# The reciprocal roots of the norms: from ScalarE's square root to VectorE alone

## The chip, the cores and the metric

The kernel runs on one core of a Trainium2 chip. Five engines of that core work side by side, each through its own queue in order: TensorE (PE, matrix products into PSUM), VectorE (DVE), ScalarE (ACT), GpSimd (POOL) and SyncE (SP, which issues the transfers). The metric is the time of one launch on the device in microseconds; lower is better.

## The reference

Four transformer layers over 512 tokens of width 1024, batch 1, in float32. Layers 0 and 1 are a block with sparse attention (a top-k of keys, then compressed and selected keys) and a gated feed-forward network; layers 2 and 3 are a block with gated linear attention (GLA) and sliding-window attention, each with a squared-ReLU network of width 4096. What matters here is the norm that stands ahead of every product, behind some of them, and inside GLA:

```
def rms_norm(x, w):
    xf = x.astype(jnp.float32)
    y = xf * lax.rsqrt(jnp.mean(xf * xf, axis=-1, keepdims=True) + NORM_EPS)
    return (y * w.astype(jnp.float32)).astype(x.dtype)
```

For each token (or each token and head) it needs one number, the reciprocal root of a mean of squares.

## The kernel before

The activations are kept transposed: `x` is a tile of 128 partitions by 8 chunks by 512 tokens. Weights come from HBM in units of 128x1024, once each. A float32 product is made of three matmuls in the fast float32 form: weights and activations are split into a rounded part `hi` and a rest `lo` (`mm3`, L195; lines L198 to L200). So each unit of weights costs an ACT copy (`whi`, L188) and a subtraction (`wlo`, L175) on DVE or, where the caller says `eng=self.G`, on POOL, in pieces of 256 columns.

A norm goes in these steps. ACT squares the activations (L224), DVE adds them up (L226, L230), and a matmul with a column of ones sums over the partitions (`sums_out`, L235), so that the sum of each token stands in one partition, one column for each block of 128 tokens. `meanv` (L254, or L257, or by hand at L963 and L1409) makes the mean plus epsilon in a tile `mv` of 1 to 8 columns. `rsqrt` (L238) makes the reciprocal root in a tile `rsq`. Either the root is used as a factor for each partition, when a product is moved out of PSUM (L1042, L1110, L1620) or a tile is scaled (L794, L796), or `bcast` (L269) spreads it over all partitions: DVE multiplies it into an identity (L273), a matmul with ones copies it to every row (L277), and ACT moves that to SBUF as `rb` (L280).

`rsqrt` before: ACT takes the square root of `v` into a tile `rs_s` (L243), DVE takes the reciprocal (L244), and one Newton step on DVE sharpens it (L245 to L247): y becomes y times (1.5 - 0.5 v y y). The square root needs ACT's table of that function; ACT's other functions here with a table of their own are Exp, Silu, Tanh and Ln, and where the next function's table isn't there, a load of it (ACT_TABLE_LOAD) stands ahead of it in ACT's queue.

`rsqrt` is called 26 times in a run: for the memory's norm (L567) and the norm of `ckv` (L1105) in layer 0, ahead of every mixer and every network (through `rms`, L260, and at L765, L976), for both roots at the start of layer 2 (L1411), for each of GLA's four heads (L1615), behind the mixers and networks of layers 2 and 3 (`post_norm`, L818 and L821), and for the output rows at the very end (`result_of`, L964).

The order of the work is written by hand with `weave` and `steps`, which mix lists of steps in a given ratio. The final order of each engine's queue comes from a planner that lists the instructions by a simulated time line:

```
    with tile.TileContext(nc, schedule_with_timeline_sim=True) as tc:
        body(tc, args)
```

Of the kernel before, what the change touches and what calls it, by code (L numbers as in the profile page):

```python
# [9 lines left out]

F32 = mybir.dt.float32
F32R = mybir.dt.float32r
AF = mybir.ActivationFunctionType
ALU = mybir.AluOpType
AX = mybir.AxisListType

P = 128
# [92 lines left out]
class Core:  # L110
# [20 lines left out]
    def pair(self, name):  # L131

        return self.blk([P, 2, S], F32R, name)

# [42 lines left out]
    def split(self, src, hi, lo, eng=None):  # L177
        self.A.activation(hi, src, AF.Copy)  # L178
        self.lo(lo, src, hi, eng)
# [4 lines left out]
    def wunit(self, src, n=1024, eng=None):  # L184
        raw = self.wraw()
        hi, lo = (self.wp.tile([P, 1024], F32R, tag=t, name=self.uid(t), bufs=NW) for t in ("whi", "wlo"))
        self.nc.sync.dma_start(raw[:, :n], src)
        self.A.activation(hi[:, :n], raw[:, :n], AF.Copy)  # L188
        w = 256 if eng is self.G else 512
# [13 lines left out]
    def sums(self, srcs, sl=ALL, scale=None):  # L203
# [7 lines left out]
        else:  # L211
            for c, x in enumerate(srcs):
                o = self.t2() if c else acc
                self.A.activation(o[:, sl], x, AF.Square, scale=scale(c))
                if c:
# [3 lines left out]
    def sums_in(self, pairs, out, st=None, last=True):  # L219

        st = {} if st is None else st
        for x in pairs:
            o = self.t2([P, 2, 256])
            self.A.activation(o, x, AF.Square)  # L224
            if "a" in st:
# [11 lines left out]

    def rsqrt(self, v, n):  # L238

        s = self.sm([P, 16], "rs_s", 2)  # L240
        y = self.sm([P, 16], "rsq", 6)
        t = self.sm([P, 16], "rs_t", 2)
        self.A.activation(s[:, :n], v, AF.Sqrt)  # L243
        self.V.reciprocal(y[:, :n], s[:, :n])  # L244
        self.V.tensor_tensor(t[:, :n], y[:, :n], y[:, :n], ALU.mult)  # L245
        self.V.scalar_tensor_tensor(t[:, :n], t[:, :n], -0.5, v, ALU.mult, ALU.mult)
        self.V.scalar_tensor_tensor(y[:, :n], t[:, :n], 1.5, y[:, :n], ALU.add, ALU.mult)  # L247
        return y[:, :n]

    def meanv(self, ssum, n, dim, mul=None):  # L250
# [18 lines left out]
    def bcast(self, y, nb=NB, out=None):  # L269
# [8 lines left out]
        if out is None:  # L278
            out = self.sm([P, S], "rb", 2)[:, :n]
        self.A.activation(out, ps[:, :n], AF.Copy)  # L280
        return out
# [10 lines left out]
    def act_half(self, gain, sl):  # L292

        ts = [self.blk([P, 2, 2, 256], F32R, "ah") for _ in range(4)]
        out = [(ts[c // 2][:, c % 2, 0], ts[c // 2][:, c % 2, 1]) for c in range(KC)]
# [64 lines left out]
    def tr4(self, srcs, tag="gm"):  # L360

        ps = self.psum(tag, F32R)
        for j, x in enumerate(srcs):
# [3 lines left out]
    def stack_steps(self, jobs, tag="gm", eng=None, hi="A"):  # L367


        def task(*job):  # L370
# [3 lines left out]
            def s0():  # L374
                src = job[0][:] if len(job) == 3 else job[0][job[1]][:, b]
                v["st"] = st = self.t2([P, 4, 2, 64], F32R)
                src4 = src.rearrange("p (h d) -> p h d", d=64)
# [19 lines left out]
    def k_stack(self, src, out):  # L397

        sh, sl = self.t2([P, NB, 2, 64], F32R), self.t2([P, NB, 2, 64], F32R)
        src = src[:, :, None, :].to_broadcast([P, NB, 2, 64])  # L400
# [1492 lines left out]
```

## Time and profile before

| | us |
|---|---|
| median of 3 timed runs | 2369.89 |
| lowest and highest | 2369.83, 2370.73 |
| the profiled execution | 2373.13 |
| its span, first to last instruction | 2371.4 |

The profiled execution is one run of its own, taken with the profiler; all rows are of it. The page gives for each engine its busy time, its share of the span and its number of instructions. The mean granted clock of PE over the span is 0.992 of full speed. Rows of the timeline begin with the start and the duration in us, then engine, line, operation and tiles; an idle time of the engine before the instruction and what ended it stand in brackets at the end.

### The profile page before, as it was taken

To read this page: it belongs to the slowest core of one execution; us is meant where nothing else is said; L and a number is where in the kernel's file an instruction comes from. 1 tells how busy PE (TensorE), PEld (TensorE's weight loads), DVE (VectorE), ACT (ScalarE), POOL (GpSimd) and SP (SyncE) were. 2 spreads that over 40 slices of the span, in tenths; PEclk is the share of its full clock that TensorE was granted. 3 is DMA by queue.
4 is the path that set the end of the run, shared out by engine and by line. 5 is a ranking of instruction groups with operands and counts; after the bars stand their busy time and mean duration, and the time that the engine had idled before them with its cause. 6 is when DMAs were issued, how large, how long until landed. Compare 5 with 4: busy or idle time off the path is not lost.

```text
span 2371.4 us, 35348 instructions
## 1 busy us (share of the span) xinstructions
PE 2323.4 (98%) x13390; PEld 2006.0 (85%) x13390; DVE 1436.0 (61%) x2978; ACT 1130.5 (48%) x2121; POOL 476.2 (20%) x706
## 2 busy tenths in 40 slices
PE   8899999999999999999999999999999999999998
PEld 8788988888997879888888998988888877988886
DVE  5996655455667676555456446844446796644446
ACT  6677522222457675222226566633325686533233
POOL 2756000000137730000001660000000161000000
PEclk9999999999999999999999999999999999999999
DMA  5213422223330114222222214523234413522234
GB/s 179 72 37 101 145 101 93 98 98 98 101 132 21 58 43 141 98 98 98 98 94 77 81 63 149 171 92 104 89 104 154 146 61 125 167 87 102 97 98 142
DMA packets 68300, 243.88 MB, mean 103 GB/s; under 512 B 7569, under 2 KB 7825, under 8 KB 68130
## 3 DMA queue, kind: packets, MB, share of 16 engines
q1 hardware_dynamic: 68130, 241.62, 30.7%
q8 instruction: 106, 1.74, 0.3%
q14 instruction: 64, 0.52, 0.1%
HBM read 239.50 MB, written 2.10 MB: 102 GB/s over the span
## 4 chain that ended last, share of the span: by engine, by line
PE 89%; DVE 6%; ACT 3%; DMA 1%; issue 1%; POOL 0%; SPq 0%; DVEq 0%; ACTq 0%; POOLq 0%
PE ps L199 11%; PE ps L200 11%; PE ps L198 11%; PE tr L198 10%; PE tr L199 10%; PE tr L200 10%; PE gm L198 3%; PE gm L200 3%; PE gm L199 3%; PE acc L529 2%; PE more L198 2%; PE more L200 2%; PE more L199 2%; PE tr L451 2%; PE ps L424 1%; PE ps L425 1%
## 5 line engine op out<-in xcount | busy, mean ns | idle before, releaser
L188 ACT ACTIVATE whi<-raw 128x1024 fp32r<-128x1024 f32 (+1 forms) x443 | 466.4, 1054 | 863.0 <-PE ps L199 221.0
L175 DVE TENSOR_TENSOR wlo<-raw,whi 128x512 fp32r<-128x512 f32 x744 | 524.9, 747 | 322.9 <-ACT whi L188 321.4
L175 POOL TENSOR_TENSOR wlo<-raw,whi 128x256 fp32r<-128x256 f32 x284 | 219.7, 805 | 272.2 <-ACT whi L188 184.2
L200 PE MATMUL ps<-act,wlo 128*128 128x512 f32 (+1 forms) x712 | 257.1, 361 | 0.5 <-DVE wlo L175 0.4
L198 PE MATMUL ps<-act,whi 128*128 128x512 f32 (+1 forms) x712 | 257.0, 361 | 0.2 <-DVE m L863 0.2
L199 PE MATMUL ps<-act,whi 128*128 128x512 f32 (+1 forms) x712 | 256.8, 361 | 0.1
L200 PE MATMUL tr<-act,wlo 128*128 128x512 f32 (+1 forms) x640 | 231.7, 362 | 0.0
L198 PE MATMUL tr<-act,whi 128*128 128x512 f32 (+1 forms) x640 | 231.4, 362 | 0.2 <-ACT whi L188 0.2
L199 PE MATMUL tr<-act,whi 128*128 128x512 f32 (+1 forms) x640 | 231.3, 361 | 0.0
L731 POOL TENSOR_TENSOR sm_s<-sm_s,sm_s 128x512 f32<-128x512 f32 x40 | 51.6, 1289 | 532.0 <-DVE sm_s L730 532.0
L200 PEld LDWEIGHTS ps<-act,wlo 128*128 128x128 f32 x712 | 134.4, 189 | 21.1 <-DVE wlo L175 0.7
L198 PEld LDWEIGHTS ps<-act,whi 128*128 128x128 f32 x712 | 134.3, 189 | 20.8 <-issue 0.6
L199 PEld LDWEIGHTS ps<-act,whi 128*128 128x128 f32 x712 | 134.1, 189 | 20.7 <-DVE act L302 0.3
L198 PEld LDWEIGHTS tr<-act,whi 128*128 128x128 f32 x640 | 120.8, 189 | 18.7 <-ACT whi L188 0.3
L199 PEld LDWEIGHTS tr<-act,whi 128*128 128x128 f32 x640 | 120.9, 189 | 18.5
L200 PEld LDWEIGHTS tr<-act,wlo 128*128 128x128 f32 x640 | 120.8, 189 | 18.3
L445 POOL TENSOR_TENSOR sm_s<-sm_s,nm_r 128x256 f32<-128x256 f32 (+2 forms) x172 | 104.3, 622 | 50.8 <-DVE nm_r L479 19.3
L178 ACT ACTIVATE hid<-sm_s 128x512 fp32r<-128x512 f32 x88 | 55.7, 632 | 109.5 <-DVE sm_s L884 58.0
L198 PE MATMUL gm<-whi,act 128*128 128x256 f32 (+1 forms) x360 | 103.3, 289 | 1.3 <-ACT rb L280 0.6
L200 PE MATMUL gm<-whi,act 128*128 128x256 f32 (+1 forms) x360 | 102.6, 287 | 0.0
L199 PE MATMUL gm<-wlo,act 128*128 128x256 f32 (+1 forms) x360 | 102.1, 286 | 0.0
L199 PE MATMUL ps<-wlo,hid 128*128 128x512 f32 x256 | 99.7, 390 | 0.0
(661 smaller groups left out, 5803.8 us busy)
## 6 DMA issues: line engine op xcount, KB each, us to landing
raw<-in_w_down SPq DMA_DIRECT2D x124, 512.0 KB, 3.3
raw<-in_w_ffn SPq DMA_DIRECT2D x96, 512.0 KB, 3.3
raw<-in_w_up SPq DMA_DIRECT2D x80, 512.0 KB, 3.4
raw<-in_w_o SPq DMA_DIRECT2D x32, 512.0 KB, 3.3
raw<-in_w_glao SPq DMA_DIRECT2D x16, 512.0 KB, 3.4
raw<-in_w_swa SPq DMA_DIRECT2D x16, 512.0 KB, 3.3
raw<-in_w_swao SPq DMA_DIRECT2D x16, 512.0 KB, 3.3
raw<-in_w_dsa SPq DMA_DIRECT2D x14, 512.0 KB, 3.9
```

Source lines behind the costliest of these rows:

```text
L175: (eng or self.V).tensor_tensor(out, src, hi.bitcast(F32), ALU.subtract)
L178: self.A.activation(hi, src, AF.Copy)
L188: self.A.activation(hi[:, :n], raw[:, :n], AF.Copy)
L198: mm(out, l[0], r[0], start=start, stop=False)
L199: mm(out, l[0], r[1], start=False, stop=False)
L200: mm(out, l[1], r[0], start=False, stop=stop)
L424: self.T.matmul(out, q[:, t], k[0][:, k0:k0 + n], start=True, stop=False)
L425: self.T.matmul(out, q[:, t], k[1][:, k0:k0 + n], start=False, stop=True)
L445: self.G.tensor_tensor(p, p, r.to_broadcast([P, p.shape[-1]]), ALU.mult)
L451: self.T.transpose(ps[:, s], p[:, s], self.ident)
L529: return self.T.matmul(acc[e * 64:e * 64 + 64, t0:t0 + p[e].shape[-1]], v[e], p[e], start=start and i == 0, stop=stop and i == n - 1)
L731: self.G.tensor_tensor(u, u, t, ALU.mult)
```

## The change

`rsqrt` no longer uses ACT. DVE takes the bits of `v` as an integer, multiplies by -0.5 and adds 1597463007, and the bits of that integer, read as float32, are a first guess of the reciprocal root. Three Newton steps of the same three operations as before follow. So the tile `rs_s`, the Sqrt and the reciprocal go; one operation on bits and two Newton steps more come. Its callers are untouched.

```
-        s = self.sm([P, 16], "rs_s", 2)
         y = self.sm([P, 16], "rsq", 6)
         t = self.sm([P, 16], "rs_t", 2)
-        self.A.activation(s[:, :n], v, AF.Sqrt)
-        self.V.reciprocal(y[:, :n], s[:, :n])
-        self.V.tensor_tensor(t[:, :n], y[:, :n], y[:, :n], ALU.mult)
-        self.V.scalar_tensor_tensor(t[:, :n], t[:, :n], -0.5, v, ALU.mult, ALU.mult)
-        self.V.scalar_tensor_tensor(y[:, :n], t[:, :n], 1.5, y[:, :n], ALU.add, ALU.mult)
+        self.V.tensor_scalar(y[:, :n].bitcast(I32), v.bitcast(I32), -0.5, 1597463007.0, ALU.mult, ALU.add)
+        for _ in range(3):
+            self.V.tensor_tensor(t[:, :n], y[:, :n], y[:, :n], ALU.mult)
+            self.V.scalar_tensor_tensor(t[:, :n], t[:, :n], -0.5, v, ALU.mult, ALU.mult)
+            self.V.scalar_tensor_tensor(y[:, :n], t[:, :n], 1.5, y[:, :n], ALU.add, ALU.mult)
         return y[:, :n]
```

(`I32` is a new name for the 32-bit integer type.)

## Rows read from the trace of the kernel before

**Rows 1.** The page: busy us, share of the span, instructions of an engine.
```profile
PE 2323.4 (98%) x13390; PEld 2006.0 (85%) x13390; DVE 1436.0 (61%) x2978; ACT 1130.5 (48%) x2121; POOL 476.2 (20%) x706
```

**Rows 2.** The page: the chain that ended last, shares by engine.
```profile
PE 89%; DVE 6%; ACT 3%; DMA 1%; issue 1%; POOL 0%; SPq 0%; DVEq 0%; ACTq 0%; POOLq 0%
```

**Rows 3.** Waits of PE: who waited for whom, us in total, times, longest.
```profile
PE gm L277 <- DVE t L273: 3.9, 2, 2.1
...
PE tr L451 <- ACT pt L517: 2.0, 1, 2.0
...
PE gm L198 <- ACT rb L280: 0.6, 1, 0.6
...
PE ps L198 <- ACT qT L178: 0.4, 1, 0.4
...
PE tr L1622 <- DVE sg L1620: 0.3, 1, 0.3
```

**Rows 4.** Line L243, its table loads: ns min/median/max, first and last start.
```profile
L243 ACT ACT_TABLE_LOAD  x12: 1283/1283/1283, 23.9 to 1975.9; - x12
```

**Rows 5.** Timeline of DVE, a call beside which POOL is idle.
```profile
264.98 0.15 DVE L254 TENSOR_SCALAR mv<-gm 128x2 f32<-128x2 f32 x1
...
265.60 0.16 DVE L245 TENSOR_TENSOR rs_t<-rsq 128x2 f32<-128x2 f32 x1
265.79 0.16 DVE L246 SCALAR_TENSOR_TENSOR rs_t<-rs_t,mv 128x2 f32<-128x2 f32 x1
...
266.18 0.42 DVE L273 TENSOR_TENSOR t<-consts,rsq 128x256 f32<-128x256 f32 x1
```

**Rows 6.** Timeline of DVE, the last two calls, merged.
```profile
2363.97 0.27 DVE L963 TENSOR_SCALAR pns<-pns 128x1 f32<-128x1 f32 x2
...
2365.16 2.74 DVE L968 SCALAR_TENSOR_TENSOR xt<-f,rsq,xt 128x512 f32<-128x512 f32 x4
```

**Rows 7.** Timeline of DVE and POOL, the second layer-3 norm.
```profile
1877.80 0.16 DVE L254 TENSOR_SCALAR mv<-gm 128x2 f32<-128x2 f32 x1 [0.17 <-PE gm L235]
...
1878.91 0.65 DVE L246 SCALAR_TENSOR_TENSOR rs_t<-rs_t,mv 128x2 f32<-128x2 f32 x1
...
1880.28 0.91 DVE L273 TENSOR_TENSOR t<-consts,rsq 128x256 f32<-128x256 f32 x1
...
1878.12 5.73 POOL L175 TENSOR_TENSOR wlo<-raw,whi 128x256 fp32r<-128x256 f32 x8 [76.41 <-ACT whi L188]
```

**Rows 8.** Timeline of DVE, the memory's norm in layer 0.
```profile
57.35 0.16 DVE L254 TENSOR_SCALAR mv<-more 128x2 f32<-128x2 f32 x1 [1.29 <-PE more L235]
...
59.65 0.54 DVE L246 SCALAR_TENSOR_TENSOR rs_t<-rs_t,mv 128x2 f32<-128x2 f32 x1
60.23 0.66 DVE L247 SCALAR_TENSOR_TENSOR rsq<-rs_t,rsq 128x2 f32<-128x2 f32 x1
```

**Rows 9.** Timeline of DVE, the norm of `ckv`.
```profile
91.39 0.47 DVE L246 SCALAR_TENSOR_TENSOR rs_t<-rs_t,mv 128x4 f32<-128x4 f32 x1
```

**Rows 10.** Busy us by window: length, PE, PEld, DVE, ACT, POOL, PE's clock, DMA.
```profile
98.00:112.00 14.00, 11.79 (x94) 11.18 (x95) 14.00 (x38) 8.64 (x20) 11.84 (x13) 1.00 0.12 36
```

**Rows 11.** Timeline of DVE and POOL, GLA's second output norm.
```profile
1381.23 0.35 DVE L254 TENSOR_SCALAR mv<-oss 128x4 f32<-128x4 f32 x1 [1.70 <-ACT t L1609]
...
1384.39 0.16 DVE L247 SCALAR_TENSOR_TENSOR rsq<-rs_t,rsq 128x4 f32<-128x4 f32 x1
...
1378.73 5.60 POOL L175 TENSOR_TENSOR wlo<-raw,whi 128x256 fp32r<-128x256 f32 x8 [2.17 <-ACT whi L188]
```

**Rows 12.** Timeline of ACT and PE, layer 1's network norm; then a window.
```profile
835.48 1.28 ACT L243 ACT_TABLE_LOAD   x1
...
837.00 1.28 ACT L430 ACT_TABLE_LOAD   x1
...
840.24 1.28 PE L451 MATMUL tr<-consts,sm_s 128*128 128x128 f32 x7 [2.05 <-ACT pt L517]
...
842.00:844.00 2.00, 2.00 (x6) 0.98 (x7) 0.92 (x5) 1.72 (x6) 0.00 (x0) 0.50 0.00 0
```

More of the change, by code (lines that the diff above doesn't have):

```diff
@@ L12 @@
 F32R = mybir.dt.float32r
+I32 = mybir.dt.int32
 AF = mybir.ActivationFunctionType
```

## The prediction

> **What bounds the kernel now.** I read the page's busy lines first: TensorE (PE) is busy for 98% of the span, VectorE (DVE) 61%, ScalarE (ACT) 48% [rows 1]. The chain that ended last says the same: 89% of it is PE, 6% DVE, 3% ACT [rows 2]. So nearly everything that the norms do on the other engines lies beside matmuls, and a change to them shows only where PE stands still for them, or after its last matmul. I took those places from the waits of PE: of the rows that touch a norm, `gm L277` (the matmul of `bcast`) waits for DVE's `t L273` twice, 3.9 us in all; `tr L451` waits 2.0 us for ACT's `pt`, `gm L198` 0.6 us for ACT's `rb`, `ps L198` 0.4 us for ACT's `qT` and `tr L1622` 0.3 us for DVE's `sg` [rows 3]. The other calls of `rsqrt` have no PE idle behind them. 26 calls are made in a run, by my count in the code.
>
> **What each call loses and gains.** Before: one Sqrt on ACT, then four DVE operations. After: ten DVE operations, each needing the one before it. Twelve of the Sqrts bring a table load of 1.283 us [rows 4], and further loads put back what Sqrt had displaced. All of these go, and so does the hop to ACT and back.
>
> With GpSimd (POOL) quiet, a dependent small DVE operation follows the one before in (266.18 - 265.60) / 3 = 0.193 us. From the end of `mv` (264.98 + 0.15 = 265.13) to the start of its reader at 266.18 the old way takes 1.05 us, its table load having been made ahead of the wait [rows 5]. The new way takes 0.03 + 10 x 0.193 = 1.96 us. So a quiet call of which ACT is not late comes out 0.9 us later. Where ACT reached the Sqrt late, it comes out earlier.
>
> With POOL busy it is another matter. In the layer-3 norm POOL runs eight subtractions from 1878.12 on, 5.73 us, or 0.72 us each. There L246 starts at 1878.91, and the reader of the result, two steps on, at 1880.28: 0.685 us a step in place of 0.193, and L246 itself shows 0.65 us where it takes 0.16 elsewhere [rows 5, 7]. So nine Newton operations beside such a stream cost up to 6 us instead of 1.8. That is the centre of my forecast: the six net additional operations are cheap by themselves, but some land where POOL splits weights.
>
> The trace here has a two-input operation taking about one POOL instruction per step, and the single-input `mv` at 1381.23 takes 0.35 us against 0.15 quiet [rows 5, 11]. The Trainium skill, page "SBUF — State Buffer", section "SBUF: two separate sides", says that VectorE and GpSimd contend for one port pair that is locked for a whole instruction, by VectorE operations with two SBUF inputs and by those in a two-port mode. The rows agree for two inputs. By the rule the new first operation, single-input in SBUF, could be held too: up to one POOL instruction more at the four places below, up to 2.8 us, and the sum would be 11.3 us. I keep the sum without it.
>
> **The places, one by one** (time before, my value, its bounds).
>
> 1. Memory norm, layer 0. `mv` ends at 57.51, the root at 60.89, with L247 taking 0.66 us: POOL is busy [rows 8]. PE already waits here for `t L273` [rows 3]. The new chain can start at 57.55; 0.2 + 9 x 0.58 to 9 x 0.685 (the step between the two, rows 7 and 8) puts its end at 63.0 to 63.9, and another DVE instruction stands in between. +3.0. Lowest -1.4 (quiet steps from 57.55), highest +3.5.
>
> 2. The norm of `ckv`, layer 0. Here DVE also runs the top-k search, and soon after it is busy for all 14.00 us of 98 to 112 [rows 10], so what is added before that is paid whole. L246 takes 0.47 us here [rows 9]. Six more operations: 6 x 0.47 = +2.8. Lowest 6 x 0.16 = +1.0, highest 6 x 0.685 = +4.1.
>
> 3. FFN norm, layer 1. ACT is held from 835.48 to 838.28 by the load for Sqrt, Sqrt, and the load for the softmax's Exp; PE then stands 2.05 us until 840.24 because `pt` isn't evacuated, and from 842 to 844 its granted clock is 0.50, the 1.2 GHz level [rows 12]. Without the loads ACT is 2.8 us earlier, more than the gap: -2.05, and the two slow microseconds give back 1.0 if the clock does not fall. Next late is DVE, which gets six more operations between its softmax minima; I give 0.3 back. -2.8. Bounds -3.1 (all of it) and 0 (DVE late in ACT's stead).
>
> 4. Norms at the start of layer 2. ACT's evacuations wait for the root, and PE for the broadcast behind them, 0.6 us [rows 3]. A quiet call: +0.9. Bounds 0 and +0.9.
>
> 5. Second head's output norm in layer 2. `mv` ends 1381.58; POOL's eight subtractions end at 1378.73 + 5.60 = 1384.33, 0.70 us each [rows 11]. About four Newton operations go at that pace, five at 0.193: the root at 1385.3 against 1384.55. +0.8. PE waits 0.3 us there already, so it has nothing spare. Lowest -0.3 (that wait gone), highest +3.5 (all nine at 0.70).
>
> 6. Second half of the layer-3 norm. `mv` ends 1877.96. The first Newton operation ends where the old L245 did, before 1878.91; then come seven at 0.685 until POOL's stream ends (1878.12 + 5.73 = 1883.85), then one quiet: 1883.9, against 1880.24. The product behind it, 0.91 us beside POOL, is 0.42 without [rows 5, 7]. +3.2 at PE, which waits there 2.1 us now [rows 3]. Lowest -0.3 (quiet), highest +3.7 (half a microsecond more at the lower clock level, which rows 12 show after a PE idle of this size).
>
> 7. Layer 3's output product waits 0.4 us for ACT's `qT` [rows 3], which stands behind a load for Sqrt. -0.4; at worst 0.
>
> 8. The tail. After the last matmul PE is out of it. The first of the two means starts at 2363.97 and the product that uses the roots at 2365.16; both chains interleave on DVE, so they count once [rows 6]. New: 2363.97 + 0.2 + 10 x 0.193 = 2366.10. +1.0, bounds +0.9 and +1.2.
>
> The other norms I cost at nothing, since PE has matmuls queued that do not need them. Without that cover each would cost 0.9 us.
>
> The sum: 3.0 + 2.8 - 2.8 + 0.9 + 0.8 + 3.2 - 0.4 + 1.0 = +8.5 us. The profiled execution took 2373.13 us, span 2371.4, so it would be 2381.6. The timed median is 2369.89, 3.2 us lower; I lay the difference on that: **2378.4 us**. Adding the bounds gives -3.6 to +16.9.
>
> **Rivals.**
>
> A. The chains do not meet POOL's streams. The kernel's order comes from a simulated schedule, and with no hop to ACT the steps may stand earlier or the weight splits later. Then places 1, 5 and 6 end at -1.4, -0.3, -0.3, place 2 at +1.0, the rest as above: -1.4 + 1.0 - 2.8 + 0.9 - 0.3 - 0.3 - 0.4 + 1.0 = -2.3 us, 2367.6: not slower, within what can be told. For it: a plan that is made anew. Against: POOL starts when ACT's `whi` is ready, which no norm holds back; DVE already lost time to it in places 1, 2, 5 and 6. It decides from the point where fewer than about three of the four meet.
>
> B. ACT's relief is what counts. The twelve loads for Sqrt and five that put a table back (the one at 837.00 is such) are 17 x 1.283 = 22 us of ACT. With A's chains, place 3 at -3.1 and the 0.6 us behind ACT's `rb` gone instead of 0.9 added, it is -4.1; a little more in stalls too short to be listed makes -5, 2364.9. Against: ACT is busy 48% [rows 1], and most loads ran while it waited. The Trainium skill, page "ScalarE: Activation LUTs", section "What ACT_TABLE_LOAD costs", gives 2.66 us for each switch, drain included; 17 of them would be an estimate of 45 us, and I would put this rival at 0.2. The trace disagrees: the load at 835.48 takes 1.28 us and the next one, after the Sqrt, is at 837.00 [rows 12], so there is no such drain. I leave it at 0.08.
>
> C. The longer chains are spread out among other DVE work. Ten steps instead of four can each stand behind a weight split on DVE; a norm that is hidden now then runs out of its cover. For it: at 57 and at 1381 a call already takes about 3 us from `mv` to root [rows 8, 11]. Price: the forecast and one such 0.685 us step for each of nine steps at one place, +6, so 2384.4.
>
> **How the numbers follow.** Forecast 0.55, A 0.22, B 0.08, C 0.15. About 0.2%, or 4.7 us, is what can be told from no change here: 2365.2 to 2374.6. Slower: 0.15 of C and nine tenths of the forecast, 0.65. Same: the rest of the forecast and nearly all of A, 0.25. Faster: B and a little of A, 0.10. The range is 2367.5, about A's value, to 2386, just under the upper bounds; the forecast's own range is 2373 to 2384.
>
> **What would show it.** No Sqrt on ACT, and 17 table loads fewer. DVE's Newton operations with durations of 0.4 to 0.7 us at places 1, 2, 5 and 6 and 0.16 elsewhere. PE's wait for `t L273` at 3.9 + 6 us in all. The wait of `tr L451` for `pt` gone. About 1 us more from the last matmul to the end. I am wrong if the Newton operations are short throughout, or if PE's waits for `t L273` do not grow.

## The result and the profile after

The changed kernel takes 2391.97 us (median of 4 runs, 2390.90 to 2393.51) against 2370.31 (2369.83 to 2371.72) for the kernel before on the same chip: 21.7 us slower, ratio 1.0089, 95% interval 1.0078 to 1.0101. I had said 2378.4 and a range up to 2386. The direction was right, the size was not: +21.7 in place of +8.5.

Lines ahead of `rsqrt` have moved down by one (the matmuls are L199 to L201, `wlo` is L176), those behind it have not; the chain of operations in `rsqrt` is L243 (bits), L245 to L247 (three times). The profiled execution has a span of 2389.7 us; its table loads are 13 in place of 31, 18 fewer (I had counted 17). The busy line and the chain's shares of the page hardly differ from [rows 1, 2]:

```profile
PE 2325.3 (97%) x13390; PEld 2005.9 (84%) x13390; DVE 1468.4 (61%) x3134; ACT 1105.0 (46%) x2077; POOL 474.2 (20%) x706
...
PE 89%; DVE 6%; ACT 4%; issue 1%; DMA 1%; POOL 0%; SPq 0%; DVEq 0%; ACTq 0%; POOLq 0%
```

DVE has 32.4 us more work, half as much again as the 21.7. PE's waits tell more (who waited for whom, us in total, times, longest), here those of the changed kernel, behind them two of the kernel before that [rows 3] leave out:

```profile
PE gm L277 <- DVE t L273: 8.4, 2, 5.6
...
PE more L364 <- DVE t L176: 3.6, 1, 3.6
PE more L1111 <- DVE t L1110: 3.5, 2, 3.1
PE gm L364 <- DVE t L176: 2.7, 1, 2.7
...
PE tr L1622 <- DVE sg L1620: 2.2, 1, 2.2
```

```profile
PE more L364 <- DVE t L175: 2.9, 1, 2.9
...
PE more L1111 <- DVE t L1110: 1.0, 1, 1.0
```

Against [rows 3]: the wait for the norm's broadcast (`t L273`) went from 3.9 to 8.4, that for `sg` (the second GLA head) from 0.3 to 2.2, and `tr L451` for `pt` (2.0) is gone. `more L1111` waits for a product with the root of `ckv`; that wait was 1.0 before and is 3.5. The two waits for `t L176` are the splits of transposed tiles in layer 0; no norm is named there, and one of them (`more L364`) was there before, with 2.9.

The chain itself is as forecast where POOL is quiet, 1.97 us from the end of `mv` to the root's, and long beside POOL. Timeline of DVE, a quiet call, then the memory norm [rows 8] and POOL beside it, then the second layer-3 norm [rows 7] and POOL (start us, duration us, engine, line, operation, tiles):

```profile
1350.14 0.17 DVE L254 TENSOR_SCALAR mv<-oss 128x4 f32<-128x4 f32 x1 [5.15 <-ACT t L1609]
1350.35 0.17 DVE L243 TENSOR_SCALAR rsq<-mv 128x4 int32<-128x4 int32 x1
...
1352.12 0.16 DVE L247 SCALAR_TENSOR_TENSOR rsq<-rs_t,rsq 128x4 f32<-128x4 f32 x1
...
55.49 0.16 DVE L254 TENSOR_SCALAR mv<-more 128x2 f32<-128x2 f32 x1 [1.29 <-PE more L236]
55.68 0.53 DVE L243 TENSOR_SCALAR rsq<-mv 128x2 int32<-128x2 int32 x1
56.25 0.64 DVE L245 TENSOR_TENSOR rs_t<-rsq 128x2 f32<-128x2 f32 x1
...
62.38 0.16 DVE L247 SCALAR_TENSOR_TENSOR rsq<-rs_t,rsq 128x2 f32<-128x2 f32 x1
...
54.76 2.81 POOL L176 TENSOR_TENSOR wlo<-raw,whi 128x256 fp32r<-128x256 f32 x4
...
1890.50 0.58 DVE L243 TENSOR_SCALAR rsq<-mv 128x2 int32<-128x2 int32 x1
1891.11 0.64 DVE L245 TENSOR_TENSOR rs_t<-rsq 128x2 f32<-128x2 f32 x1
...
1894.51 0.16 DVE L247 SCALAR_TENSOR_TENSOR rsq<-rs_t,rsq 128x2 f32<-128x2 f32 x1
...
1888.82 5.64 POOL L176 TENSOR_TENSOR wlo<-raw,whi 128x256 fp32r<-128x256 f32 x8 [78.94 <-ACT whi L189]
```

Last, layer 0 in windows of 30 us (length, PE busy with its number of matmuls, PE's granted clock, DMA share and GB/s), before and then after:

```profile
50.00:80.00 30.00, 24.46 (x179) 0.94 0.33 106
80.00:110.00 30.00, 28.19 (x200) 0.95 0.12 36
110.00:140.00 30.00, 28.26 (x240) 1.00 0.22 72
140.00:170.00 30.00, 26.88 (x209) 0.94 0.11 36
```

```profile
50.00:80.00 30.00, 22.07 (x148) 0.89 0.25 78
80.00:110.00 30.00, 24.91 (x168) 0.89 0.15 47
110.00:140.00 30.00, 25.11 (x194) 0.89 0.12 39
140.00:170.00 30.00, 28.29 (x224) 0.94 0.20 68
```

PE stands more (7.4 us less busy in the four windows together), and a larger share of it runs at the 1.2 GHz level: the clock is at half for 10.2 us of this stretch before and for 23.9 us after. In the profile after, matmuls of 256 columns follow each other in 0.21 us at the half level and in 0.12 at the full one, so the 13.7 us more can have cost about 6 us of the 10.4 lost in layer 0 (below) at most (an estimate from these figures).

I measured where the time goes by the start of the k-th matmul in both traces (each has 13390), and call the difference the lag. Times of places are those of the kernel before. Layer 0 (to 170 us of the kernel before) adds 10.4 us, the stretch from 1380 to 1870 us 4.9, the 30 us around the layer-3 norm 4.5, the rest of layer 3 2.0; from 170 to 1380 us 4.6 come back. One caution: kernels below that differ only later have the same instructions in the same order in layer 0, and yet take -3.5, -0.9 and +0.4 us there against the profile of before. So a lag in layer 0 can be off by 3 to 4 us. All lags are against one profiled execution of 2373.13 us, about 2.7 us above the usual median of that kernel.

### The profile page after: what moved, and what is told of

It is laid out like the page before. It is cut to its first block, busy times and chain, and to the rows that moved or that the text cites. A ratio compares the mean times of both kernels' runs of the same rounds, so it can differ in the third digit from the quotient of the medians.

```text
span 2389.7 us, 35476 instructions
## 1 busy us (share of the span) xinstructions
PE 2325.3 (97%) x13390; PEld 2005.9 (84%) x13390; DVE 1468.4 (61%) x3134; ACT 1105.0 (46%) x2077; POOL 474.2 (20%) x706
## 4 chain that ended last, share of the span: by engine, by line
PE 89%; DVE 6%; ACT 4%; issue 1%; DMA 1%; POOL 0%; SPq 0%; DVEq 0%; ACTq 0%; POOLq 0%
PE ps L200 11%; PE ps L201 11%; PE ps L199 11%; PE tr L199 10%; PE tr L200 10%; PE tr L201 10%; PE gm L199 3%; PE gm L200 3%; PE gm L201 3%; PE acc L529 2%; PE more L200 2%; PE more L201 2%; PE more L199 2%; PE tr L451 2%; PE ps L424 1%; PE ps L425 1%
## 5 line engine op out<-in xcount | busy, mean ns | idle before, releaser
L176 DVE TENSOR_TENSOR wlo<-raw,whi 128x512 fp32r<-128x512 f32 x744 | 527.2, 750 | 327.0 <-ACT whi L189 325.7
L176 POOL TENSOR_TENSOR wlo<-raw,whi 128x256 fp32r<-128x256 f32 x284 | 217.9, 800 | 288.1 <-ACT whi L189 200.1
L199 PE MATMUL ps<-act,whi 128*128 128x512 f32 (+1 forms) x712 | 257.3, 362 | 0.2 <-DVE m L863 0.2
L201 PE MATMUL ps<-act,wlo 128*128 128x512 f32 (+1 forms) x712 | 257.2, 361 | 0.0
L201 PE MATMUL tr<-act,wlo 128*128 128x512 f32 (+1 forms) x640 | 231.9, 362 | 0.0
L199 PE MATMUL tr<-act,whi 128*128 128x512 f32 (+1 forms) x640 | 231.7, 362 | 0.0
L199 PEld LDWEIGHTS ps<-act,whi 128*128 128x128 f32 x712 | 134.6, 189 | 21.1 <-issue 0.6
L201 PEld LDWEIGHTS ps<-act,wlo 128*128 128x128 f32 x712 | 134.9, 190 | 20.2
L201 PEld LDWEIGHTS tr<-act,wlo 128*128 128x128 f32 x640 | 121.0, 189 | 18.7 <-DVE wlo L176 0.2
L199 PEld LDWEIGHTS tr<-act,whi 128*128 128x128 f32 x640 | 121.2, 189 | 18.4
L199 PE MATMUL gm<-whi,act 128*128 128x256 f32 (+1 forms) x360 | 103.6, 290 | 1.3 <-DVE v L1425 0.5
L201 PE MATMUL gm<-whi,act 128*128 128x256 f32 (+1 forms) x360 | 102.0, 285 | 0.0
```

Of the source, the lines that this page charges most:

```text
L176: (eng or self.V).tensor_tensor(out, src, hi.bitcast(F32), ALU.subtract)
L199: mm(out, l[0], r[0], start=start, stop=False)
L201: mm(out, l[1], r[0], start=False, stop=stop)
```

## The experiments

All were timed beside the kernel before; differences are against its median on the same chip, intervals belong to ratios. "Steps" below are the chain's DVE operations.

### How many steps, and with or without the square root

`one_step`: the changed kernel with one Newton step in place of three, so with as many DVE operations as before and no Sqrt (its root is far less sharp).

```
-        for _ in range(3):
+        for _ in range(1):
```

> The changed kernel with one Newton step after the first guess in place of three: four DVE operations a call, as many as before the change, and no Sqrt. (It leaves out two of the three steps, so its roots are rougher; its time is what is wanted.) Theory 'steps' (the six additional dependent operations cost the time, whether by GpSimd's instructions or by standing behind other work): the cost goes and what the missing Sqrt gives back stays, about 2366 to 2368 us. Rival 'plan' (the cost is that the order of all queues was made anew without the Sqrt): it stays near 2385 to 2392.

Measured: 2369.84 us, ratio 1.0001 (0.9992 to 1.0010).

`sqrt_three_steps`: the kernel before, its Newton step made three times.

```
+        for _ in range(3):
             self.V.tensor_tensor(t[:, :n], y[:, :n], y[:, :n], ALU.mult)
```

> The kernel before with Sqrt and reciprocal kept and two Newton steps added, so ten DVE operations a call and all table loads. Theory 'steps': the cost of the changed kernel and on top of it what the loads cost, which the changed kernel saves: 2394 to 2398 us. Rival 'plan': 2370 to 2376.

Measured: 2393.25 us, ratio 1.0095 (1.0082 to 1.0108). So the loss comes with the six added operations: with them the time is the same to 1.3 us (21.7 and 23.0 more than before) whether the square root stays or goes, and without them 18 table loads fewer gain nothing that can be measured. That speaks against rival B; it is not clean, since each kernel has an order of its own. It does not tell yet why six small operations in 26 calls cost 22 us: with two more steps in each of the old chains the planner also makes a new order, and `one_step` still lost 7.3 us in layer 0 and won it back later.

### Which calls

`bits_at_four`: the new way only at places 1, 2, 5 and 6 (8 calls). `sqrt_at_four`: the old way only there.

```
-    def rsqrt(self, v, n):
+    def rsqrt(self, v, n, bits=False):        # True at the calls named; sqrt_at_four the other way round
...
```

> The new way only where the trace shows the Newton operations beside GpSimd's weight splits: the memory's norm, the norm of ckv, GLA's output norms, and the two norms at the start of layer 3 (8 of the 26 calls); the old way elsewhere. Theory 'lock' (the cost lies where these operations meet GpSimd): PE's lag in the changed kernel's trace grows there by 12.8 (layer 0) + 1.4 + 4.3 = 18.5 us, so about 2389. Rival 'spread' (the steps stand behind other DVE work everywhere, so the cost goes by the number of calls): 2370.3 + 21.7 x 8 / 26 = 2377.

> The reverse: the old way at those 8 calls and the new way at the other 18. Theory 'lock': about 2371 to 2373, since elsewhere gains and losses of the lag nearly cancel. Rival 'spread': 2370.3 + 21.7 x 18 / 26 = 2385.

Measured: 2386.70 us, ratio 1.0070 (1.0058 to 1.0082); and 2373.89 us, ratio 1.0016 (1.0008 to 1.0025). The 8 calls where POOL is busy hold 16.4 us, the other 18 calls 3.6. These are the places that I had named; I had put 9.8 us on them (3.0 + 2.8 + 0.8 + 3.2).

`bits_mem`, `bits_ckv`, `bits_l3`: the new way at one place alone (1, 2, or both norms at the start of layer 3), by the same argument.

> The new way only in the memory norm of layer 0 (one call), the square root everywhere else. Theory 'lock' (the added steps cost what POOL's stream makes them cost, once, where they stand): the Newton operations last 0.5 to 0.7 us, PE's wait for the broadcast at 57 to 61 us grows by about 3 us, later matmuls keep that lag of 3 to 4 us, time 2373 to 2374.5. Rival 'plan' (a change of a norm re-makes the order of DVE's work in the rest of layer 0, and that is where most of the 10 to 13 us go): the lag is 3 us after 61 us and 8 us or more at 165 us, time 2378 or more.

> The new way only in the norm of ckv in layer 0 (one call). Theory 'lock': no lag before 90 us, six more steps of 0.45 to 0.66 us, +2.8 to +4 us at 98 us, kept to 165 us; time 2373 to 2374.5. Rival 'plan': lag of 8 us or more at 165 us with the same chain, because the order of DVE's work behind it turns round; time 2378 or more.

> The new way only in the two norms at the start of layer 3 (two calls). Theory 'lock': five or more of the second call's Newton operations last 0.65 us, the chain from the mean to the root takes 4.5 to 5 us in place of 2.3, PE waits 5 to 5.6 us for the broadcast in place of 2.1; time 2373 to 2374.5. Rival 'steps' (ten dependent steps cost 0.9 us more than the old way wherever they stand): 2371.2.

Measured: 2379.29 us, ratio 1.0031 (1.0019 to 1.0042); 2378.20 us, 1.0029 (1.0019 to 1.0039); 2375.14 us, 1.0013 (1.0004 to 1.0022), against 2371.65. Each layer-0 norm alone costs about 7 us, more than twice my term; the layer-3 norms cost 3.5, near my 3.2. In `bits_mem` the lag grows by 3.0 us at the memory norm (from -1.1 at 60 us to 1.9 at 66), as "lock" has it, and to 7.4 by 118 us, as "plan" has it: more comes where nothing was changed. (3.1 us of it are left at the end of this profile, 2376.27 us, which is the shortest of the kernel's six runs.) The longest common order of DVE's instructions in the first 170 us, compared by operation and tile, leaves out 74 of 384 in `bits_mem` and 107 in the changed kernel: these stand elsewhere.

`bits_late`: the new way only in the late half of layer 1. I meant place 3 by it.

> The new way only in the late half of layer 1 (one call), the place where a load for Sqrt, the Sqrt and the load for Exp hold ACT and PE then stands 2.05 us. The forecast's term of place 3, by itself: PE's wait for pt at 840 us gone, DVE's six more operations give a little back, -2.8 us, bounds -3.1 and 0: 2367.2 to 2370.3, no lag elsewhere. Rival: DVE is late in ACT's stead, or the re-made order loses it elsewhere: 2370 to 2373.

Measured: 2370.43 us, ratio 1.0004 (0.9995 to 1.0013), and the wait is still there:

```profile
PE tr L456 <- ACT pt L522: 2.0, 1, 2.0
```

So the loads that hold ACT at 835 us belong to another call, the norm ahead of the network (through `rms`), and this run says nothing on term 3.

### Is it the wait for POOL?

`bits_l3_psum`: as `bits_l3`, but the iterate lies in PSUM.

```
+        z = self.lps[:, 32:32 + n]           # spare columns of the PSUM tile that held the sums
...
+        self.V.tensor_scalar(z.bitcast(I32), v.bitcast(I32), -0.5, 1597463007.0, ALU.mult, ALU.add)
+        for i in range(3):
+            self.V.scalar_tensor_tensor(t, z, -0.5, v, ALU.mult, ALU.mult)
+            self.V.tensor_tensor(t, t, z, ALU.mult)
+            self.V.scalar_tensor_tensor(y if i == 2 else z, t, 1.5, z, ALU.add, ALU.mult)
```

> As the kernel before it in this call, but the iterate y is kept in PSUM and the three products of a step are taken in another order, so that each of the nine Newton operations reads one operand from SBUF and one from PSUM in place of two from SBUF; their number and dependence are the same. Theory 'lock' (a DVE operation with two inputs in SBUF has to wait for POOL's instruction): the operations take 0.16 to 0.3 us beside POOL, the chain 2 to 2.8 us, time 2370 to 2371.8. Rival 'steps' (it is the number of dependent operations, or any DVE operation is slowed beside POOL): operations of 0.65 us, the same time as that kernel, 2373 to 2374.5.

Measured: 2372.44 us, ratio 1.0004 (0.9995 to 1.0013). The intervals of the two kernels overlap; the rows decide. The second norm's chain on DVE in `bits_l3`, and in `bits_l3_psum` with POOL's stream and PE's wait behind the chain:

```profile
1878.18 0.17 DVE L244 TENSOR_SCALAR rsq<-mv 128x2 int32<-128x2 int32 x1
1878.39 0.61 DVE L250 TENSOR_TENSOR rs_t<-rsq 128x2 f32<-128x2 f32 x1
1879.03 0.65 DVE L251 SCALAR_TENSOR_TENSOR rs_t<-rs_t,mv 128x2 f32<-128x2 f32 x1
...
1882.43 0.16 DVE L250 TENSOR_TENSOR rs_t<-rsq 128x2 f32<-128x2 f32 x1
```

```profile
1880.13 0.16 DVE L276 TENSOR_SCALAR gm<-mv 128x2 int32<-128x2 int32 x1
1880.33 0.16 DVE L278 SCALAR_TENSOR_TENSOR rs_t<-gm,mv 128x2 f32<-128x2 f32 x1
1880.52 0.16 DVE L279 TENSOR_TENSOR rs_t<-rs_t,gm 128x2 f32<-128x2 f32 x1
...
1881.88 0.16 DVE L280 SCALAR_TENSOR_TENSOR rsq<-rs_t,gm 128x2 f32<-128x2 f32 x1
...
1878.91 5.71 POOL L176 TENSOR_TENSOR wlo<-raw,whi 128x256 fp32r<-128x256 f32 x8 [76.38 <-ACT whi L189]
...
PE gm L295 <- DVE t L291: 4.7, 2, 2.9
```

POOL runs through the whole second chain, and no step of it takes over 0.17 us; the chain from `mv` to root takes 1.94 us in place of 4.83, and the lag that the place adds (1870 to 1900 us) is 0.7 us in place of 4.1. It is not the number of dependent steps: it is that a step with both operands in SBUF waits for POOL's instruction. The Trainium skill, page "SBUF — State Buffer", section "SBUF: two separate sides", states it so (VectorE operations with two SBUF inputs and GpSimd lock one port pair for a whole instruction); the trace agrees, 0.65 us against 0.16.

`all_psum` does this wherever a PSUM tile is at hand, with all ten steps (the post norms and the last norms stay in SBUF); `psum_old_post` is the same but for the post norms and the last norms, which keep the square root; `psum_two_steps` takes two Newton steps there in place of three.

```
-        r = self.rsqrt(self.meanv(self.sums_out(sl, sq), 2, D), 2)
+        r = self.rsqrt(self.meanv(self.sums_out(sl, sq), 2, D), 2, self.lps[:, 32:])
...
```

> The change as it is, with all its steps, but in the norms that have a PSUM tile at hand (memory, ckv, late half of layer 1, start of layer 2, GLA outputs, start of layer 3) the iterate y lies in PSUM, so that a Newton operation reads one operand from SBUF and one from PSUM; the post norms and the last norms stay in SBUF. Theory 'lock' (most of the 21.7 us is the wait of two-SBUF-input operations for POOL, and what that wait sets off behind it in layer 0): the chains at the four places take 2 to 2.5 us, layer 0's lag at 165 us is under 2 us, and what is left is the quiet price at a few places, the post norms (2 to 4 us) and the tail (0.6 us), less place 3: time 2370 to 2376. Rival 'steps' (ten dependent steps, or the new plan of layer 0): chains in PSUM change nothing in layer 0's lag of 8 to 12 us, time 2385 or more.

> As the kernel before it in this call, but post norms and last norms keep ScalarE's square root and one step. Theory 'lock': the lag that the post norms bring (about 2.7 us before 1870 us and 2 us at 2029 us) and the tail's 0.6 us go too, place 3 keeps its gain: 2366.5 to 2371, the same as before or a little faster. Rival 'steps': 2381 or more.

> As psum_old_post, with two Newton steps in place of three at the norms that are in PSUM. Each chain that something waits for is 3 x 0.19 = 0.6 us shorter: theory 'lock' 2365 to 2370; rival 'steps' three ninths less than its 2381 to 2385 above the kernel before, 2377 or more.

Measured, against 2370.62: 2376.58 us, ratio 1.0028 (1.0018 to 1.0039); 2375.84 us, 1.0028 (1.0018 to 1.0037); 2364.18 us, 0.9972 (0.9964 to 0.9981). With the iterate in PSUM 6.0 of the 21.7 us are left; the order is a third one, so the difference is not the chain's alone. My bound for layer 0 (a lag under 2 us) failed: it is 7.3 in `all_psum`. At 64 us, behind the memory norm, the lag is -2.9; then it goes to +5.8 by 122 us, with this window in between (length, PE busy, clock), and behind it DVE's product with the root of `ckv`:

```profile
90.90:104.56 13.66, 11.78 (x45) 0.50 0.01 1
```

```profile
92.41 2.99 DVE L1123 SCALAR_TENSOR_TENSOR t<-ms,rsq,smalls 128x128 f32<-128x128 f32 x4
```

All of it at the half level, 11.78 us of matmuls that would need about 6.6 at full clock (an estimate by the 0.12 and 0.21 us above), where the kernel before has no half-clock stretch between 83 and 154 us. PE stood 2.7, 0.6 and 0.9 us from 88 us on, for `fd` and twice for products of the `ckv` norm. No step of the chain waits for POOL there, but the product behind it does: its inputs lie in SBUF, and two of the four took 1.12 and 1.42 us beside POOL instructions of 1.13 and 1.26, the other two 0.34. The longest wait, for `fd`, is neither. What else differs is the order: 104 of DVE's 384 instructions of layer 0 are elsewhere, counted as above.

Two more forecasts failed here. The square root at the post norms and the last norms gained 0.7 us, within the noise, where I had put about 5 on them (2.7, 2 and 0.6). And one Newton step less, 0.6 us a chain by my forecast, made `psum_two_steps` 11.7 us faster than `psum_old_post`: again an order of its own.

### The chain and the order apart

The order comes from the planner's simulated time line. I held it: behind the trace of all instructions, edges without a wait chain each engine's instructions (PE, DVE, ACT, POOL, all but those of `rsqrt`) in the order of another kernel; the planner then places only the chain. In the traces of these kernels every engine's instructions outside the chain, the transfers included, stand in the wanted order from the first to the last.

```
         body(tc, args)
+        pin(tc)       # for neighbours p, q of the wanted order:
+                      # tc.add_manual_dep(q, p.name, NoSync)
```

`new_chain_old_order` is the changed kernel in the order of before, `old_chain_new_order` the reverse, `psum_old_order` is `all_psum` and `two_steps_old_order` is `psum_two_steps` in the order of before.

> The changed kernel, but on PE, DVE, ACT and POOL all instructions outside rsqrt are held by edges in the order of the kernel before; only the ten steps of each chain are placed by the planner. Theory 'chain' (the time is the price of the chain where it stands, with the waits and the clock that follow): layer 0 about +6 to +10 us, place 6 +3.5 to 5, post norms and tail +4, place 3 -3: 2382 to 2393. Rival 'order' (the re-made order costs more than half of the 21.7 us): 2370 to 2380.

> The kernel before, but all instructions outside rsqrt held in the order of the changed kernel. Theory 'chain': the order by itself costs little, 2368 to 2374. Rival 'order': 2380 or more, with layer 0 alone 6 us or more behind.

> all_psum (all ten steps, the iterate in PSUM where there is a tile for it) with all other instructions in the order of the kernel before. Theory 'lock with re-made order' (the wait for POOL is the chain's price, and what all_psum still lost in layer 0 was its own order): no lag in layer 0, post norms, tail and the quiet price at layer 2 left: 2367 to 2373. Rival 'steps' (ten dependent steps cost layer 0 its 6 us whatever the order): 2375 or more, as all_psum.

> psum_two_steps with all other instructions in the order of the kernel before. If its gain of 6 us is its chain's (no table loads at places 3 and 7, no wait for POOL at places 1, 2, 5 and 6): 2362 to 2367. If it is the luck of its order: 2367 to 2371.

Measured, against 2370.57 (time: difference of medians in us; lags in us by stage, from one profile each):

| | time | ratio, interval | to 170 us | 170 to 1380 | 1380 to 1870 | 1870 to 1900 | to 2364 |
|---|---|---|---|---|---|---|---|
| changed kernel | +21.7 | 1.0089 (1.0078 to 1.0101) | +10.4 | -4.6 | +4.9 | +4.5 | +2.0 |
| new chain, old order | +12.2 | 1.0049 (1.0036 to 1.0061) | +6.5 | -2.6 | +3.6 | +3.8 | -0.3 |
| old chain, new order | +14.6 | 1.0057 (1.0045 to 1.0069) | +2.2 | -0.9 | +1.4 | +3.1 | +2.6 |
| PSUM chain, old order | +2.8 | 1.0008 (1.0000 to 1.0017) | -4.8 | -4.8 | -0.5 | -1.9 | +7.7 |
| two steps, old order | +0.1 | 1.0001 (0.9992 to 1.0009) | -1.9 | -4.0 | -0.7 | -2.0 | +7.2 |

The lags of a row do not add up to its time, because each row compares one execution with one other: the profile of "old chain, new order" is 3.0 us under that kernel's median, that of "PSUM chain, old order" 2.4 under, that of "new chain, old order" 2.9 over, and the one of before 2.6 over. So only 8.4 of the 14.6 us have a stage. The times decide; a stage shows where to look.

Both theories had a part right, and each was wrong as a whole. The chain where it stands costs 12.2 us, just inside the range of "chain", not the whole; the new order with the old chain costs 14.6, which "chain" had excluded, but layer 0 is 2.2 us behind and not the 6 that "order" wanted. They overlap: together 21.7, not 26.8. And in the old order the PSUM chain takes 9.4 of the 12.2 us away; layer 0 is then 4.8 us in front, about as far as `bits_late` with nothing changed there. Not run: the kernel before held in its own order, which would show what the edges cost by themselves.

How an order costs is plain at the layer-3 norm. `old_chain_new_order` has the old chain, but the sums and the splits ahead of it stand otherwise, the mean starts later behind PE's matmuls, and PE has run out of work by then; timeline of DVE, and PE's waits:

```profile
1882.67 0.16 DVE L264 TENSOR_SCALAR mv<-gm 128x2 f32<-128x2 f32 x1 [1.17 <-PE gm L238]
1883.44 0.17 DVE L254 RECIPROCAL rsq<-rs_s 128x2 f32<-128x2 f32 x1 [0.61 <-ACT rs_s L253]
...
PE gm L287 <- DVE t L283: 5.8, 2, 4.0
```

4.0 us where [rows 3] have 2.1. In layer 3's post norm the steps of the changed kernel stand one by one behind weight splits,

```profile
2024.56 0.16 DVE L246 SCALAR_TENSOR_TENSOR rs_t<-rs_t,mv 128x2 f32<-128x2 f32 x1
2025.35 0.15 DVE L247 SCALAR_TENSOR_TENSOR rsq<-rs_t,rsq 128x2 f32<-128x2 f32 x1
2026.15 0.15 DVE L245 TENSOR_TENSOR rs_t<-rsq 128x2 f32<-128x2 f32 x1
2026.22 1.29 DVE L176 TENSOR_TENSOR wlo<-raw,whi 128x512 fp32r<-128x512 f32 x2
...
2036.23 0.15 DVE L247 SCALAR_TENSOR_TENSOR rsq<-rs_t,rsq 128x2 f32<-128x2 f32 x1
```

12.3 us from mean to root. That looks like the cause of the 2 us lost there, but with the new chain in the old order nothing is lost (-0.3), and with the old chain in the new order 2.6 are: it is the order of the rest. Both kernels in the new order have the same waits of PE behind this norm, for `act` (below, the changed kernel, then the old chain in the new order) and 0.7 us for `x`; neither kernel in the old order has them.

```profile
PE ps L200 <- DVE act L302: 1.6, 2, 1.3
```

```profile
PE ps L202 <- DVE act L312: 1.6, 2, 1.3
```

`psum_old_order` has a loss of its own, the +7.7 at the end: the planner spread the chain of one norm, ahead of layer 3's network, between weight splits, the iterate holds a PSUM tile until its last step, and PE's transposes of `x` wait for that tile.

```profile
PE gm L975 <- DVE rsq L259: 6.1, 1, 6.1
```

`ten_steps_hidden` and `best` were to take this away: `psum_old_order` and `two_steps_old_order` with the square root at the norms ahead of the squared-ReLU networks, the post norms and the last norms, in the order of before.

```
-            self.bcast(self.rms(sl), 2, v["rb"][:, sl])
+            self.bcast(self.rms(sl, None, True), 2, v["rb"][:, sl])
```

> psum_old_order, but the norms ahead of the squared-ReLU networks, the post norms and the last norms keep ScalarE's square root; the others have all ten steps, with the iterate in PSUM. Old order. Theory 'lock': with the wait for POOL gone, and no PSUM tile held at 2028 us, ten steps in place of five cost nothing, and the loads for Sqrt that are gone give back 3 to 4 us: 2364 to 2368. Rival 'steps': 2370 to 2375.

> As the kernel before it in this call, with two Newton steps in place of three where the iterate is in PSUM. Theory 'lock': 2362 to 2366, as psum_two_steps or a little better, so that the old order is as good as the lucky one. Rival 'order' (the gain of psum_two_steps was its order's): 2367 to 2371.

Measured: 2374.73 us, ratio 1.0018 (1.0008 to 1.0028); 2373.62 us, ratio 1.0013 (1.0004 to 1.0022), against 2371.07. I changed the wrong call, the norm ahead of the gated networks: the wait at `gm L975` stays (6.1 and 5.5 us), so the question that they were made for is not answered. The call that I did change is that of place 3, and `ten_steps_hidden` shows what it is worth: PE's wait for `pt` is back, which `psum_old_order` does not have.

```profile
PE tr L474 <- ACT pt L540: 2.1, 1, 2.1
```

The best version that ran is `psum_two_steps` in the planner's own order, 2364.18 us, faster than the kernel before by 0.28% (0.19 to 0.36%). In the old order it takes 2370.69 us, which lies where I had put it if the gain was the luck of its own order (2367 to 2371). But its lags up to 1900 us sum to about the same in both orders (-8.6 in the old against -8.8 us); what the old order lacks is the 7.2 us at the end.

## Why the prediction was wrong

**The step that failed** is one that I did not cost: the sum has a term for each of eight places and takes all other instructions as staying where they are. The planner makes the whole order anew when a chain changes, which I wrote in rival A and there only as a gain. On top of the chain it costs 9.5 us (21.7 - 12.2), with the old chain 14.6. No rival of mine had that mechanism. None of my signs could tell it either, for they came true: long steps beside POOL, waits for `t L273` of 8.4 us where I had 9.9, the wait for `pt` gone, 0.6 us more at the end.

**What the sum did cover,** the chain in the old order, measured +12.2 (interval about 8.5 to 14.5) against +8.5, which is at the edge. Term by term by the lags of `new_chain_old_order`, one profile, with its waits of PE:

```profile
PE gm L287 <- DVE t L283: 9.5, 3, 5.3
...
PE more L1121 <- DVE t L1120: 2.4, 1, 2.4
PE tr L1632 <- DVE sg L1630: 2.2, 1, 2.2
...
PE gm L202 <- ACT rb L290: 1.3, 1, 1.3
```

- Place 1 (+3.0): the chain takes 6.88 us from `mv` to root against 3.4; I had 5.5 to 6.4. The lag grows by 3.0 us there and to 4.6 by 85 us, because the clock is at half for 6.8 us behind the longer gap, 3.4 before. I had a half-clock cost at place 6's bound only.
- Place 2 (+2.8): 2 to 3 us between 85 and 120 us. Right in this order. The 7 us that `bits_ckv` costs alone are chain and new order together. I had said that no other call has PE idle behind it; PE's wait for this product was 1.0 us before (`more L1111`) and is 2.4 here.
- Place 3 (-2.8): -2.2. The mechanism was right; PE's next wait is 1.4 us for the norm's own broadcast.
- Place 4 (+0.9): the gap behind `rb` is 1.3 in place of 0.6, but a half-clock stretch of 6.8 us that [rows 3] do not show is gone there, and the lag falls by 0.8. Wrong in sign.
- Place 5 (+0.8): +3.5. Mis-sized, at its upper bound: PE stands 2.2 us for `sg`, and the clock goes to half for 3.4 us behind it. In the changed kernel the root comes 4.9 us behind `mv`; I had 3.7, four held steps.
- Place 6 (+3.2): +3.9; a wait of 5.3 us for 2.1, and 6.8 us of half clock for 3.4.
- Place 7 (-0.4): -0.7, of which 0.4 come back at once; there is no wait for `qT`. Place 8 (+1.0): 11.2 us from PE's end to the span's for 10.2; in the changed kernel 10.8.

With the order held, these eight make up the 12.5 us by which that profile's span is longer, to about 0.2 us: the other norms did cost nothing.

**The rule that I did not follow** for the first operation: it takes 0.53, 0.45, 0.67 and 0.58 us at the four places against 0.17 quiet, 1.55 us more in all. (In `bits_l3` it took 0.17 beside POOL; it began there 0.08 us ahead of one of POOL's instructions.) The Trainium skill's page "SBUF — State Buffer", section "SBUF: two separate sides", lets a single-input operation in a two-port mode be held too; I had left it out of the sum, and at most 2.8 would have come with it. The trace agrees that a single-input operation can be held; which mode it ran in no run shows.

**The rivals.** A is out: the chains met POOL at all four places. B is out: the time rose with the relief of ACT, and `one_step` shows no gain. C named something that is there, steps spread between other work, and a cost of the right sign, but its reason fell. In layer 3 PE loses by the order of the rest. At the norm of `ckv` the steps stand one by one between those of the top-k search in the old order too, and PE waits 2.4 us with the iterate in SBUF but 1.1 with it in PSUM, as long as before; ten spread steps cost nothing there once POOL does not hold them. This line is of `psum_old_order`:

```profile
PE more L1134 <- DVE t L1133: 1.1, 1, 1.1
```

Still open: why the planner's new order loses in layer 0. I saw PE's gaps and the half-clock stretches behind them, not which choice makes them; and 6 of the 14.6 us of the order alone have no place in its profile.

## What to carry to other kernels

An added operation has two prices: its own place, and the order that the planner makes of everything else; hold the old order by edges to tell them apart before explaining a loss or a gain. A small dependent chain on VectorE beside a GpSimd stream pays one GpSimd instruction per step unless one operand lies in PSUM. And a gap of PE costs more than its length where a half-clock stretch follows it (place 1: 3.0 us at the gap, 4.6 behind the stretch).

## What the runs showed of the hardware

- With one operand in PSUM no step waited for POOL (0.16 us each, against 0.65 with both in SBUF), nor did the first one, whose only input is in SBUF and whose output is in PSUM: 0.16 against 0.58 with the output in SBUF (`bits_l3_psum`, the changed kernel).
- 18 table loads of 1.283 us each, taken off ACT, gave no measurable time in `one_step` (ratio 1.0001, in an order of its own). At the one place where PE waited behind them, the wait of 2.0 us went.
- The same instructions in the same order took up to 4 us more or less in the first 170 us from one kernel's profile to another's.
